# Gated DeltaNet trunk on one core: merge products later in the order, copies off GpSimd, the memory norm moved to K's and V's eviction

## The chip, the core and the metric

One core of one Trainium2 chip runs the whole kernel. Its engines are TensorE (PE; its weight loads are shown as PEld), VectorE (DVE), ScalarE (ACT), GpSimd (POOL) and SyncE (SP), which issues the DMAs. The metric is the device time of one launch in microseconds (us), lower is better.

## What is computed

Two decoder layers over 512 positions of 1024 channels, all float32. Layer 0 mixes tokens with gated DeltaNet, layer 1 with a Conformer convolution; each then cross-attends into a fixed memory of 256 positions and applies a squared-ReLU MLP. The parts that the change touches:

```python
# gated DeltaNet, 8 heads of 128, chunks of 64 positions
qkv = silu(causal_depthwise_conv(h @ w_in[:, :3072], w_conv))      # 4 taps
a_mat = eye(64) + where(strict, (k*beta) @ k.T * decay, 0)
sol = triangular_solve(a_mat, concat([v*beta, k*beta*exp(g_cum)]))
...                                                                # a scan over chunks carries the state
o = rms(o) * out_norm * silu(z);  h = h + o @ w_out
# memory cross-attention
kv = (rms_norm(mem, xa_mem_norm) ) @ w_kv                          # K and V of 256 memory positions
```

## The kernel before

Activations lie with the channels on the partitions, 128 channels by 512 positions per tile. Every float32 product is done as three matmuls in a split form: an operand is split into a high and a low part (`split`, L264; `wsplit`, L203, for weights: an ACT copy makes `wh`, DVE subtracts to make `wl`), and `mm3` (L227) multiplies high by high, high by low and low by high.

**Order.** The DeltaNet stage is written as a list of "mains" (L1136 to L1166), pieces of TensorE work that are issued one after another, and a table of "sides": `S.at(i, rank, f)` (L281) has `f` issued behind main `i`, lower ranks first. Mains 0 to 3 are the first key head and the gates' columns; then, for heads 0 to 3 (group 0) and heads 4 to 7 (group 1), come projections of k, q, z and v (`DN_ORDER`), two mains for each head; the 16 units of the cross-attention's K and V (`kv_unit`, L779) are mains 66 to 81. The places of the sides are constants by hand (`MG`, `FS`, `REC`, `K2`, ..., L1317 to L1346). A tile framework turns the issue order into one instruction order for each engine when the kernel is built: an instruction that its own reckoning has ready may go ahead of earlier ones. On the chip each engine then works its list in that fixed order and waits at the head of it.

**One group of heads.** `ev_k`, `ev_q`, `ev_v` evict a projection from PSUM (a multiply by the norm's `rb` on DVE) and apply the four convolution taps in `conv_head` (L441): tap 0 on ACT, of the others the first `npool` as an ACT multiply into `cvq` and a GpSimd add, the rest as a DVE multiply-add. v used npool 3. `k2` makes the lower-triangular matrices, `fs_in` (L517) copies their 32x32 diagonal blocks into `DB` on ACT, `fs_begin` and `fs_steps` (L527, L535) solve them by forward substitution on DVE, 31 steps of two instructions (`fst`, `X`). `fs_end` (L545) transposes the result twice into `TB` and `UB`. `mg_pre` (L554) clears `x0`, `u0` and the diagonal blocks of `bt` on GpSimd; `mg_a` (L563) copies the blocks of `TB` into `x0` on ACT and those of `UB` into `u0` on GpSimd, four copies of 32x128 each for a head. `mg_w`, `mg_y`, `mg_y`, `mg_end` (L574 to L599) are the merge products on TensorE that join the four 32-blocks to a 128-block inverse `U`. `v2` (L612) transposes v, and `rec` (L636) runs the recurrence over four 128-position chunks, three steps each, with `o_gate` and `o_norm` behind it. `head_out` (L719) transposes a head's output for the output projection "do".

**Around it.** `mem_stat` (L748) makes the memory's inverse norm `rs` and GpSimd multiplied the four memory tiles by it; `mem_gain` (L762) then applies the gain and splits. The output projection ran behind the mains (L1247 to L1260): 8 tiles `m`, each over all 8 heads. In the Conformer (L978), `CONV_SEQ` and `CONV_AFTER` place DVE's taps, their transposes ("d", `turn`), the layer norm ("l") and its output transposes ("o", `ln_out`) among the 16 K and V units of layer 1.

Of the kernel before, what the change touches and what calls it, by code (L numbers as in the profile page):

```python
# [8 lines left out]
F32 = mybir.dt.float32  # L9
# [5 lines left out]
P = 128  # L15
# [23 lines left out]
def tile_trunk(ctx, tc, xT, memT, prm_d, adt_d, bdw_d, tap_d, fin_d, w_ab, w_kq, w_v, w_z, w_dno, w_pw1, w_pw2,  # L39
# [29 lines left out]
    def tt(e, o, a, b, op):  # L69
        e.tensor_tensor(out=o, in0=a, in1=b, op=op)  # L70

# [59 lines left out]
    ind = const([P, 4], "ind")  # L131
    dve.tensor_reduce(out=ind, in_=ident.rearrange("p (x c) -> p c x", c=4), op=ALU.add, axis=AX.X)
    headm = const([P, 8], "headm")
    headx = const([P, 32], "headx")
    dve.tensor_reduce(out=headx, in_=ident.rearrange("p (x c) -> p x c", c=4), op=ALU.add, axis=AX.X)
    dve.tensor_reduce(out=headm, in_=headx.rearrange("p (a h) -> p h a", h=8), op=ALU.add, axis=AX.X)
    eps_rms = const([P, 1], "eps_rms")
# [65 lines left out]
    def wsplit():  # L203
        u = ws["split"]
        ws["split"] += 1
        while ws["load"] <= u:
            wload()
        raw = ws["raw"].pop(u)
        h = wp.tile([P, 1024], F32R, tag="wh", name=nm("wh"), bufs=NW)
        lo = wp.tile([P, 1024], F32R, tag="wl", name=nm("wl"), bufs=NW)  # L210
        act.copy(h, raw)  # L211
        (kind, i, *j), hf = order[u]
        gp = kind == "pw1" or j and kind in "KV" and i == 1 and hf == 0
        tt(pool if gp else dve, lo, raw, h.bitcast(F32), ALU.subtract)
        ws["hl"][u] = (h, lo)
# [120 lines left out]
    class DeltaNet:  # L336
# [66 lines left out]
        def decay_const(self, gq):  # L403
            if gq == 0:
                self.R = slot(F32R, "R")
# [34 lines left out]

        def conv_head(self, ps, ti, npool):  # L441
            raw = wp.tile([P, 542], F32, tag="cv", name=nm("cv"), bufs=NCV)
            pool.memset(raw[:, 0:3], 0.0)
            tt(dve, raw[:, 3:515], ps, self.n.rb, ALU.mult)
            w = [pc("w_conv", ti * 4 + j) for j in range(4)]
            a = slot(s="cva")
            act.activation(a, raw[:, 0:512], AF.Copy, scale=w[0])
            for j in range(1, 4):
                if j <= npool:
                    b = slot(s="cvq")  # L450
                    act.activation(b, raw[:, j:j + 512], AF.Copy, scale=w[j])
# [8 lines left out]
        def ev_k(self, h):  # L460
            self.KT[h] = self.conv_head(self.ps.pop(("k", h)), 8 + h, CONV_K)

        def ev_q(self, h):
            self.M["q", h] = self.conv_head(self.ps.pop(("q", h)), h, CONV_Q)

# [51 lines left out]
        def fs_in(self, h):  # L517
# [26 lines left out]

        def fs_end(self, gq):  # L545
            X = self.fs.pop(gq)[1]
            UB = fsp.tile([P, 1024], F32, tag="fs", name=nm("UB"))
            TB = fsp.tile([P, 1024], F32, tag="fs", name=nm("TB"))
            dve.transpose(out=TB, in_=X.rearrange("p (i j) -> p j i", j=32))
            dve.transpose(out=UB, in_=X)  # L550
            self.fs[gq] = UB.rearrange("p (i n) -> p n i", n=32), TB.rearrange("p (i n) -> p n i", n=32)

# [9 lines left out]

        def mg_a(self, h):  # L563
            UBv, TBv = self.fs[h // 4]
            u0, x0, bt = self.M[h]
            n = slice(h % 4 * 4, h % 4 * 4 + 4)
            for b in range(4):
                bs = slice(32 * b, 32 * b + 32)
                act.copy(c4(x0)[bs, :, bs], TBv[bs, n, :])
                pool.tensor_copy(c4(u0)[bs, :, bs], UBv[bs, n, :])  # L570

# [30 lines left out]
        def ev_v(self, h):  # L602
            self.VT[h] = self.conv_head(self.ps.pop(("v", h)), 16 + h, CONV_V)

# [31 lines left out]
        def rec(self, gq, c, step):  # L636
# [8 lines left out]
            if step == 0:  # L645
                r = self.VB[gq, c]
                if c > 0:
# [100 lines left out]
    def mem_stat():  # L748
        ps = psum("mssq")
        for i in range(2):  # L750
            pe.matmul(ps[:, 0:256], ones, mem["acc"][:, i * 256:(i + 1) * 256], start=i == 0, stop=i == 1)
        sd = slot(s="msd")
        act.activation(sd[:, 0:256], ps[:, 0:256], AF.Sqrt, bias=eps_rms, scale=1.0 / 1024)
        rs = slot(s="mrs")
        dve.reciprocal(rs[:, 0:256], sd[:, 0:256])
        mem["n"] = []
        for m in mem["m"]:
            tt(pool, m.rearrange("p (k t) -> p k t", k=2), m.rearrange("p (k t) -> p k t", k=2),
               over_c(rs[:, 0:256], 2), ALU.mult)
            mem["n"].append(m)  # L760

    def mem_gain(layer, half):  # L762
# [3 lines left out]
        for j in (2 * half, 2 * half + 1):  # L766
            mh = slot(F32R, "mh")
            ml = slot(F32R, "ml")
            for i in range(2):
                ks = slice(i * 256, (i + 1) * 256)  # L770
                src = mem["n"][j][:, ks]
                g = pc(gn, 2 * j + i)
# [6 lines left out]
    def kv_unit(layer, u):  # L779
# [3 lines left out]
        if u < 8:  # L783
# [4 lines left out]
            if hf == 1:  # L788
                K.append(split(mem["ps"], "K"))
        else:  # L790
# [5 lines left out]
            if v % 4 == 3:  # L796
                for mt in range(2):
                    V[mt, g] = split(mem["ps"][mt], "V")

# [377 lines left out]
    for h in range(8):  # L1177
        uk = max(at["k", h] + 1, T_STAT + 2)
        for u, ev, d, key, lag in ((uk, D.ev_k, D.KT, h, LAG[0]), (at["q", h] + 1, D.ev_q, D.M, ("q", h), LAG[1]),
                                   (at["v", h] + 1, D.ev_v, D.VT, h, LAG[2])):  # L1180
            S.at(u, 4, ev, h)
            S.at(u + lag, 4.1, D.silu, d, key)
# [17 lines left out]
    for gq in range(2):  # L1200
        f0, nf = FS[gq]
        S.at(f0, 5, D.fs_begin, gq)
        for i in range(nf):
            S.at(f0 + i, 6, D.fs_steps, gq, i * 31 // nf, (i + 1) * 31 // nf)
        S.at(f0 + nf, 0, D.fs_end, gq)
        S.at(f0 + 1, 7, D.norm_k, gq)
        for i in range(4):
            h = 4 * gq + i
            m = MG[gq] + i * MSTEP[gq] // 2
            S.at(m, 1, D.mg_a, h)  # L1210
            S.at(f0 + nf - 4 + i, 5, D.mg_pre, h)
            for j, f in enumerate((D.mg_w, D.mg_y, D.mg_y, D.mg_end)):
                S.at(m + 1 + j, 1, f, h)
        for c in range(4):
            S.at(max(at["v", 4 * gq + 3] + V2[gq], f0 + nf), 3, D.v2, gq, c)
        n = 0
# [7 lines left out]
    for j in range(4):  # L1224
        S.at(MEM + 3 + j, 7, mem_square, j)
    S.at(MEM + 9, 3, mem_stat)
    S.at(at["kv"] - MGAIN, 6, mem_gain, 0, 0)
    S.at(at["kv"] - MGAIN + 1, 6, mem_gain, 0, 1)
    os_, xres = [], []
    for i in range(4):  # L1230
        S.at(HO + i, 6, lambda i=i: os_.append(D.head_out(i)))
    S.at(REC[1] + 6, 8, lambda: xres.extend(load_x()))
    run(mains, S)
# [9 lines left out]

    def do_w(m):
        return wnext(("do", m // 2), m % 2), psum("do")

    w0, p0 = do_w(0)  # L1247
    proj(w0, os_, p0, 0, 4)
    w1, p1 = do_w(1)
    proj(w1, os_, p1, 0, 4)  # L1250
    for i in range(4, 8):
        os_.append(D.head_out(i))
    proj(w0, os_, p0, 4, 8)
    do_ev(0, p0)
    proj(w1, os_, p1, 4, 8)
    do_ev(1, p1)
    for m in range(2, 8):
        w, ps = do_w(m)
        proj(w, os_, ps)
        do_ev(m, ps)  # L1260
    n2 = Norm("mlp_norm0")
# [18 lines left out]
    def finish(hid, cur):  # L1280
# [3 lines left out]
        for c, g in LAST:  # L1284
# [14 lines left out]
            if g == 0:  # L1299
# [43 lines left out]
CONV_AFTER = [(3, ("t", 5)), (11, ("d", 0)), (12, ("c", 4, 0, 1)), (13, ("c", 4, 2, 3)), (13, ("t", 6)),  # L1343
              (14, ("c", 5, 0, 1, 2, 3)), (14, ("t", 7)), (15, ("d", 1)), (16, ("c", 6, 0, 1, 2, 3)), (18, ("d", 2)),
              (18, ("c", 7, 0, 1, 2, 3)), (21, ("d", 3)), (21, ("l", 0))]
CONV_AFTER += [(24 + _m, ("o", _m)) for _m in range(8)]  # L1346

# [40 lines left out]
def _layout(np, i):  # L1388
# [25 lines left out]
    r["w_z"] = _pack_b(np, w[:, 3072:4096])  # L1414
    r["w_dno"] = _pack_a(np, i["dn_w_out"][0])
    r["w_pw1"] = _pack_a(np, i["cv_w_pw1"][0], [m for h in range(8) for m in (h, 8 + h)])
# [26 lines left out]
```

## Time and profile before

| what | value |
|---|---|
| median of 3 runs (lowest to highest) | 1579.48 us (1578.74 to 1582.63) |
| the profiled execution: its time / the span of its instructions | 1581.38 us / 1579.7 us |
| mean granted TensorE clock | 0.983 of full speed |
| DVE busy / ACT busy / POOL busy | 879.1 us / 655.7 us / 237.1 us |
| DeltaNet stage with K and V of layer 0 | 0 to about 370 us |
| output projection, cross-attention, MLP of layer 0 | about 370 to 880 us |
| Conformer with K and V of layer 1 | about 880 to 1075 us |

A time in the views of the trace counts from the first instruction. "L578 PE" is an instruction that line 578 issues on TensorE; `xN` is a count. In the list of waits, each row has who waited, for whom, the sum in us, how often, and the longest. In the table of windows the columns are the window, its length, the busy time of PE, PEld, DVE, ACT and POOL, then the granted clock (PEclk), the DMA's share and GB/s. In a timeline a row has start, duration, engine, line, operation, tiles and shape, and in brackets the idle time of that engine just before and what ended it.

### The profile page before, as it was taken

To read this page: it belongs to the slowest core of one execution; us is meant where nothing else is said; L and a number is where in the kernel's file an instruction comes from. 1 tells how busy PE (TensorE), PEld (TensorE's weight loads), DVE (VectorE), ACT (ScalarE), POOL (GpSimd) and SP (SyncE) were. 2 spreads that over 40 slices of the span, in tenths; PEclk is the share of its full clock that TensorE was granted. 3 is DMA by queue.
4 is the path that set the end of the run, shared out by engine and by line. 5 is a ranking of instruction groups with operands and counts; after the bars stand their busy time and mean duration, and the time that the engine had idled before them with its cause. 6 is when DMAs were issued, how large, how long until landed. Compare 5 with 4: busy or idle time off the path is not lost.

```text
span 1579.7 us, 19402 instructions
## 1 busy us (share of the span) xinstructions
PE 1535.3 (97%) x7622; PEld 1293.8 (82%) x7622; DVE 879.1 (56%) x1296; ACT 655.7 (42%) x1003; POOL 237.1 (15%) x262
## 2 busy tenths in 40 slices
PE   7998997999999999999999999999999999999998
PEld 5886885898888888888888888978888888888887
DVE  5886878566455444343435499864545443433441
ACT  5655573745344433231324332264444432322332
POOL 1226124502111100000001541212112000000000
PEclk8999999799999999999999999999999999999999
DMA  4221112153221233233224534542213232223231
GB/s 153 81 78 51 60 50 97 51 176 107 93 67 59 89 107 94 94 97 103 93 94 158 171 126 130 181 140 96 80 40 99 92 103 95 94 97 103 93 107 54
DMA packets 51115, 156.17 MB, mean 99 GB/s; under 512 B 6608, under 2 KB 8912, under 8 KB 51024
## 3 DMA queue, kind: packets, MB, share of 16 engines
q1 hardware_dynamic: 51024, 154.93, 30.0%
q8 instruction: 60, 0.98, 0.2%
q14 instruction: 31, 0.25, 0.0%
HBM read 151.76 MB, written 2.10 MB: 97 GB/s over the span
## 4 chain that ended last, share of the span: by engine, by line
PE 78%; DVE 10%; ACT 4%; issue 2%; POOL 2%; DMA 2%; SPq 1%; DVEq 0%; POOLq 0%; ACTq 0%
PE up L229 7%; PE up L231 7%; PE up L230 7%; PE dn L231 6%; PE dn L229 6%; PE dn L230 6%; DVE ca L73 3%; PE q L229 2%; PE xo L230 2%; PE q L231 2%; PE q L230 2%; PE xo L231 2%; PE xo L229 2%; PE pw L229 1%; PE pw L230 1%
## 5 line engine op out<-in xcount | busy, mean ns | idle before, releaser
L211 ACT CAST wh<-raw 128x1024 fp32r<-128x1024 f32 x248 | 260.5, 1051 | 688.8 <-PE dn L230 190.4
L70 DVE TENSOR_TENSOR wl<-raw,wh 128x1024 fp32r<-128x1024 f32 x224 | 276.7, 1236 | 123.5 <-ACT wh L211 122.2
L229 PE MATMUL up<-xh,wh 128*128 128x512 f32 x512 | 200.4, 391 | 0.0
L231 PE MATMUL up<-xh,wl 128*128 128x512 f32 x512 | 199.4, 389 | 0.0
L230 PE MATMUL up<-xl,wh 128*128 128x512 f32 x512 | 199.4, 389 | 0.0
L230 PE MATMUL dn<-ul,wh 128*128 128x512 f32 x448 | 174.4, 389 | 0.0
L231 PE MATMUL dn<-uh,wl 128*128 128x512 f32 x448 | 174.4, 389 | 0.0
L229 PE MATMUL dn<-uh,wh 128*128 128x512 f32 x448 | 174.4, 389 | 0.0
L70 DVE TENSOR_TENSOR h<-dn,h 128x512 f32<-128x512 f32 x56 | 41.8, 747 | 163.3 <-PE dn L231 163.3
L73 DVE SCALAR_TENSOR_TENSOR rl<-up,rb 128x512 f32<-128x512 f32 x64 | 44.2, 691 | 157.0 <-PE up L231 157.0
L70 POOL TENSOR_TENSOR sq<-sq,sq 128x512 f32<-128x512 f32 x30 | 50.2, 1674 | 468.7 <-ACT sq L304 468.7
L230 PEld LDWEIGHTS up<-xl,wh 128*128 128x128 f32 x512 | 96.2, 188 | 20.3 <-issue 0.5
L229 PEld LDWEIGHTS up<-xh,wh 128*128 128x128 f32 x512 | 96.1, 188 | 20.2 <-issue 0.5
L231 PEld LDWEIGHTS up<-xh,wl 128*128 128x128 f32 x512 | 96.1, 188 | 20.1
L230 PEld LDWEIGHTS dn<-ul,wh 128*128 128x128 f32 x448 | 84.1, 188 | 17.5
L231 PEld LDWEIGHTS dn<-uh,wl 128*128 128x128 f32 x448 | 84.1, 188 | 17.4
L229 PEld LDWEIGHTS dn<-uh,wh 128*128 128x128 f32 x448 | 84.1, 188 | 17.3
L73 DVE SCALAR_TENSOR_TENSOR ca<-x,prm,ca 128x512 f32<-128x512 f32 x120 | 88.0, 750 | 3.0 <-ACT ca L1024 1.2
L229 PE MATMUL h<-xh,wh 128*128 128x512 f32 x192 | 78.6, 409 | 2.1 <-ACT xh L297 2.1
L230 PE MATMUL h<-xl,wh 128*128 128x512 f32 x192 | 77.0, 401 | 2.0 <-DVE xl L73 2.0
L231 PE MATMUL h<-xh,wl 128*128 128x512 f32 x192 | 76.1, 396 | 0.0
L70 POOL TENSOR_TENSOR wl<-raw,wh 128x1024 fp32r<-128x1024 f32 x24 | 57.6, 2404 | 117.6 <-ACT wh L211 117.6
(330 smaller groups left out, 3073.2 us busy)
## 6 DMA issues: line engine op xcount, KB each, us to landing
raw<-w_up SPq DMA_DIRECT2D x64, 512.0 KB, 3.6
raw<-w_dn SPq DMA_DIRECT2D x64, 512.0 KB, 3.6
raw<-w_pw SPq DMA_DIRECT2D x24, 512.0 KB, 3.9
tap<-tap SPq DMA_DIRECT2D x36, 256.0 KB, 5.3
raw<-w_kq SPq DMA_DIRECT2D x16, 512.0 KB, 3.6
raw<-w_k SPq DMA_DIRECT2D x16, 512.0 KB, 4.4
raw<-w_vv SPq DMA_DIRECT2D x16, 512.0 KB, 3.7
raw<-w_q SPq DMA_DIRECT2D x16, 512.0 KB, 3.6
```

The costliest lines, as they stand in the source:

```text
L70: e.tensor_tensor(out=o, in0=a, in1=b, op=op)
L73: dve.scalar_tensor_tensor(out=o, in0=a, scalar=s, in1=b, op0=op0, op1=op1)
L211: act.copy(h, raw)
L229: pe.matmul(ps, wh, xh, start=first, stop=False)
L230: pe.matmul(ps, wh, xl, start=False, stop=False)
L231: pe.matmul(ps, wl, xh, start=False, stop=last)
```

## The change

- **Solve's end.** `fs_end` and `mg_a` are split by result: first `TB` and the copies into `x0`, now on DVE; then `UB` and the copies into `u0`, now on ACT. Both are issued right behind the last solve step (mains 29 and 58; `mg_a` was at 32 and at 61 to 63).
- **Merge products** start behind main 35 (were 33) and 67 (were 62 to 64), and each pair of heads one main later. For group 1 they so stand behind the first K units.
- **v.** `conv_head` is cut into eviction (`conv_raw`) and taps (`conv_taps`). v's taps are issued at `TAPV` (33 to 35, 66 and 67); npool for v is 1, 1, 0, 0 by head. `v2` moves from mains 36 and 67 to 39 and 71, the recurrence from 39 and 68 to 42 and 73.
- **Recurrence.** `Se` goes from GpSimd to four ACT instructions, `vn` from DVE to four ACT instructions. The `DB` copies of group 1 go from ACT to DVE.
- **Memory norm.** The four GpSimd multiplies go. The gains work on the raw memory; K's eviction multiplies by the inverse norm on DVE and then splits; V's eviction takes it as the scale of ACT's and DVE's split. Four matmuls with one output column each are added to have the norm by position. Squares go from mains 56 to 59 to mains 59 to 62, the gains four mains earlier.
- **Output projection.** It is split in two halves: heads 0 to 3 as eight mains behind the V units, added into the residual `xres` on DVE; heads 4 to 7 behind the mains. The weights are packed accordingly.
- **Start.** Three DVE reduces (L132 to L136) go to main 5. The weight splits 1 to 3 keep their place in the issue order.
- **Conformer.** The last `turn` and the layer norm move two units later (21 to 23), the outputs from 24 to 31 to 26, 27, 28, 29, 30, 30, 31, 31.

```diff
-        act.copy(h, raw)
+        ins = [act.copy(h, raw)]
+        if 0 < u < 4:
+            tc.keep_in_program_order(ins[0])
...
-        def conv_head(self, ps, ti, npool):
+        def conv_raw(self, ps):
             raw = wp.tile([P, 542], F32, tag="cv", name=nm("cv"), bufs=NCV)
             pool.memset(raw[:, 0:3], 0.0)
             tt(dve, raw[:, 3:515], ps, self.n.rb, ALU.mult)
+            return raw
+
+        def conv_taps(self, raw, ti, npool):
...
-                act.copy(db[bs, :, n:n + 4], bt[bs, :, bs].rearrange("p c i -> p i c"))
+                (dve.tensor_copy if gq else act.copy)(db[bs, :, n:n + 4], bt[bs, :, bs].rearrange("p c i -> p i c"))
...
+        def fs_end(self, gq, i):
+            X = self.fs[gq][-1]
+            t = fsp.tile([P, 1024], F32, tag="fs", name=nm("UB" if i == 0 else "TB"))
+            dve.transpose(out=t, in_=X.rearrange("p (i j) -> p j i", j=32) if i else X)
+            self.fs[gq] = {i: t.rearrange("p (i n) -> p n i", n=32), -1: X}
...
-        def mg_a(self, h):
+        def mg_a(self, h, i):
+            src, dst, n = self.fs[h // 4][i], self.M[h][i], slice(h % 4 * 4, h % 4 * 4 + 4)
             for b in range(4):
                 bs = slice(32 * b, 32 * b + 32)
-                act.copy(c4(x0)[bs, :, bs], TBv[bs, n, :])
-                pool.tensor_copy(c4(u0)[bs, :, bs], UBv[bs, n, :])
+                (dve.tensor_copy if i else act.copy)(c4(dst)[bs, :, bs], src[bs, n, :])
...
+        def tap_v(self, h):
+            self.VT[h] = self.conv_taps(self.M.pop(("v", h)), 16 + h, CONV_V[h])
...
-                        tt(pool, c4(Se), c4(self.S[gq]), over_i(hcv(egl, gq, c)), ALU.mult)
+                        for i, h, isl in hs:
+                            act.activation(Se[:, isl], self.S[gq][:, isl], AF.Copy, scale=egl[:, 4 * h + c:4 * h + c + 1])
...
-                tt(dve, c4(vn), c4(ps), over_i(hcv(self.s_neg if c else self.s_all, gq, c)), ALU.mult)
+                for i, h, isl in hs:
+                    act.activation(vn[:, isl], ps[:, isl], AF.Copy,
+                                   scale=(self.s_neg if c else self.s_all)[:, 4 * h + c:4 * h + c + 1])
...
+        mem["rs"] = slot(s="mrs")
+        dve.reciprocal(mem["rs"][:, 0:258], sd[:, 0:258])
...
-                K.append(split(mem["ps"], "K"))
+                kf = slot(s="kf")
+                tt(dve, kf.rearrange("p (k t) -> p k t", k=2), mem["ps"].rearrange("p (k t) -> p k t", k=2),
+                   over_c(mem["rs"][:, 0:256], 2), ALU.mult)
+                K.append(split(kf, "K"))
...
-    S.at(0, 4, D.decay_const, 0)
+    S.at(T_STAT + 3, 1, D.decay_const, 0)
...
+        for i in (1, 0):
+            S.at(f0 + nf, 2 - i, D.fs_end, gq, i)
+            for h in range(4 * gq, 4 * gq + 4):
+                S.at(f0 + nf, 2 - i, D.mg_a, h, i)
...
+            S.at(TAPV[h], 5, D.tap_v, h)
             for j, f in enumerate((D.mg_w, D.mg_y, D.mg_y, D.mg_end)):
-                S.at(m + 1 + j, 1, f, h)
+                S.at(MG[gq] + j + i // 2, 1, f, h)
...
+    def do_first(m):
+        ps = do_mm(0, m)
+        tt(dve, xres[m], ps, xres[m], ALU.add)
+
+    at["do"] = len(mains)
+    for m in range(8):
+        mains.append(lambda m=m: do_first(m))
...
+    for m in range(8):
+        do_ev(m, do_mm(1, m))
...
-CONV_K, CONV_Q, CONV_V = 0, 1, 3
+CONV_K, CONV_Q, CONV_V = 0, 1, (1, 1, 0, 0, 1, 1, 0, 0)
...
-MSTEP = (0, -1)
-MG = (32, 63)
-V2 = (4, 3)
-MGAIN = 4
+MG = (35, 67)
+V2 = (7, 7)
+MGAIN = 8
 HO = 76
-REC = (39, 68)
+REC = (42, 73)
 MEM = 53
+MSQ = 59
+TAPV = (33, 33, 34, 35, 66, 66, 67, 67)
```

More of the change, by code (lines that the diff above doesn't have):

```diff
@@ L404, in decay_const @@
             if gq == 0:
+                dve.tensor_reduce(out=ind, in_=ident.rearrange("p (x c) -> p c x", c=4), op=ALU.add, axis=AX.X)
+                hx = small(32)
+                dve.tensor_reduce(out=hx, in_=ident.rearrange("p (x c) -> p x c", c=4), op=ALU.add, axis=AX.X)
+                dve.tensor_reduce(out=headm, in_=hx.rearrange("p (a h) -> p h a", h=8), op=ALU.add, axis=AX.X)
                 self.R = slot(F32R, "R")
@@ L751, in mem_stat @@
             pe.matmul(ps[:, 0:256], ones, mem["acc"][:, i * 256:(i + 1) * 256], start=i == 0, stop=i == 1)
+        for mt in range(2):
+            for i in range(2):
+                o = i * 256 + mt * P
+                pe.matmul(ps[:, 256 + mt:257 + mt], mem["acc"][:, o:o + P], ones[:, 0:1], start=i == 0, stop=i == 1)
         sd = slot(s="msd")
[L753 to L760, printed above, removed]
+        act.activation(sd[:, 0:258], ps[:, 0:258], AF.Sqrt, bias=eps_rms, scale=1.0 / 1024)
+        mem["rs"] = slot(s="mrs")
+        dve.reciprocal(mem["rs"][:, 0:258], sd[:, 0:258])
     def mem_gain(layer, half):
@@ L1181, in tile_trunk @@
             S.at(u, 4, ev, h)
-            S.at(u + lag, 4.1, D.silu, d, key)
+            S.at(TAPV[h] + lag if d is D.VT else u + lag, 5.1 if d is D.VT else 4.1, D.silu, d, key)
     for gq in range(2):
@@ L1242, in do_ev @@
         n1.add(m, hn)
[L1244 to L1250, printed above, removed]
     for i in range(4, 8):
         os_.append(D.head_out(i))
[L1253 to L1260, printed above, removed]
+    for m in range(8):
+        do_ev(m, do_mm(1, m))
     n2 = Norm("mlp_norm0")
@@ L1344 @@
               (14, ("c", 5, 0, 1, 2, 3)), (14, ("t", 7)), (15, ("d", 1)), (16, ("c", 6, 0, 1, 2, 3)), (18, ("d", 2)),
-              (18, ("c", 7, 0, 1, 2, 3)), (21, ("d", 3)), (21, ("l", 0))]
-CONV_AFTER += [(24 + _m, ("o", _m)) for _m in range(8)]
+              (18, ("c", 7, 0, 1, 2, 3)), (23, ("d", 3)), (23, ("l", 0))]
+CONV_AFTER += [(_i, ("o", _m)) for _m, _i in enumerate((26, 27, 28, 29, 30, 30, 31, 31))]
 def _tiles_a(np, w):
```

57 lines of the change are left out of this document (27 added, 30 removed).

## The prediction

> **What bounds the kernel now.** I read the page's first part, then who TensorE waits for, then the windows and timelines around those waits.
>
> ```profile
> span 1579.7 us, 19402 instructions
> PE 1535.3 (97%) x7622; PEld 1293.8 (82%) x7622; DVE 879.1 (56%) x1296; ACT 655.7 (42%) x1003; POOL 237.1 (15%) x262
> ```
>
> TensorE is busy for all but 1579.7 - 1535.3 = 44.4 us. The change leaves its matmuls as they are, so it can win only idle time and the slow clock that follows it. The list of waits of TensorE, whole rows, longest first:
>
> ```profile
> PE mg L578 <- POOL msq L70: 11.2, 1, 11.2
> PE mg L578 <- ACT x L569: 6.8, 2, 6.5
> PE mg L590 <- POOL cva L70: 3.2, 1, 3.2
> PE ssq L315 <- DVE sq L70: 2.8, 1, 2.8
> PE cvT L1041 <- ACT ca L1030: 2.3, 1, 2.3
> ...
> PE lnT L1088 <- DVE cy L79: 1.9, 2, 1.5
> ...
> PE vt L615 <- DVE u L70: 1.4, 1, 1.4
> ```
>
> The merge products (mg) wait 11.2 + 6.8 + 3.2 = 21.2 us. Behind each long wait the granted clock is low:
>
> ```profile
> 26.00:30.00 4.00, 4.00 (x16) 3.32 (x16) 0.95 (x3) 1.55 (x2) 0.00 (x0) 0.59 0.37 131
> 135.00:140.00 5.00, 4.93 (x24) 4.80 (x24) 0.33 (x1) 4.83 (x12) 4.62 (x9) 0.57 0.00 0
> 276.00:285.00 9.00, 8.13 (x34) 7.26 (x35) 0.00 (x0) 8.77 (x18) 8.20 (x18) 0.50 0.01 2
> 295.00:300.00 5.00, 2.35 (x16) 2.21 (x17) 5.00 (x7) 4.92 (x11) 2.46 (x2) 0.64 0.00 0
> 300.00:310.00 10.00, 10.00 (x83) 9.57 (x82) 5.40 (x12) 4.72 (x9) 3.83 (x3) 0.67 0.33 107
> 1024.00:1027.00 3.00, 3.00 (x16) 3.00 (x16) 2.74 (x10) 0.71 (x2) 0.86 (x1) 0.53 0.40 146
> 1035.00:1040.00 5.00, 3.63 (x10) 2.78 (x11) 4.66 (x8) 3.10 (x4) 0.22 (x1) 0.71 0.36 105
> ```
>
> Busy time times (1 - clock) estimates what the slow clock costs. Start: 4.0 x 0.41 = 1.6. Group 0: 4.93 x 0.43 = 2.1. Group 1: 4.1 + 0.8 + 3.3 = 8.2. Conformer: 1.4 + 1.1 = 2.5. With the idle times, the pots are: **start** 2.8 + 0.7 (below) + 1.6 = 5.1; **group 0** 6.5 + 1.4 + 2.1 = 10.0; **group 1** 11.2 + 0.3 + 3.2 + 8.2 = 22.9; **Conformer** 2.3 + 1.9 + 2.5 = 6.7. Together 45 us.
>
> **Group 0.** The timelines of TensorE, DVE, ACT and GpSimd:
>
> ```profile
> 127.99 0.39 PE L230 MATMUL h<-xl,wh 128*128 128x512 f32 x1
> 128.22 0.39 PE L231 MATMUL h<-xh,wl 128*128 128x512 f32 x1
> 135.07 4.94 PE L578 MATMUL mg<-x,bt 128*128 128x96 f32 x24 [6.46 <-ACT x L569]
> ...
> 114.36 0.39 DVE L70 TENSOR_TENSOR X<-X,fst 128x231 f32<-128x231 f32 x1
> 116.22 1.37 DVE L70 TENSOR_TENSOR X<-X,fst 128x220 f32<-128x220 f32 x1
> 128.19 1.28 DVE L70 TENSOR_TENSOR fst<-FT,X 128x60 f32<-128x60 f32 x1
> 131.69 1.94 DVE L549 STREAM_TRANSPOSE TB<-X 128x1024 f32<-128x1024 f32 x1
> 133.67 6.78 ACT L569 COPY x<-TB 32x128 f32<-32x128 f32 x16 [0.23 <-DVE TB L549]
> 115.90 1.44 POOL L70 TENSOR_TENSOR cva<-cva,cvq 128x512 f32<-128x512 f32 x1 [22.49 <-ACT cvq L451]
> ```
>
> TensorE has nothing left but merge products at 128.6; TB exists at 133.6 and ACT copies `x0` until 140.5. Two solve steps of the same size take 0.39 and 1.37 us: the slow one runs beside GpSimd's tap add. The rows at 116.2 and 128.2 are the first and the last of six solve instructions that are slow in this way, some 6 us. The change does three things here. The products come two mains later; a main is 12 matmuls, and in the timeline they start 0.23 us apart, so 5.4 us. v's taps leave the solve's window, where GpSimd's adds fall from 12 to 2; I take 4 of the 6 us, since v's remaining taps are DVE work that can be slipped in between solve steps. And `x0` is copied on DVE:
>
> ```profile
> 36.21 0.22 DVE L360 COPY abt<-abT 128x64 f32<-128x64 f32 x1
> ...
> L73 DVE SCALAR_TENSOR_TENSOR cva<-cv,prm,cva 128x512 f32<-128x512 f32 x40 | 32.2, 806 | 13.4 <-POOL cva L70 9.1 <-ACT cva L447 3.9
> L687 ACT ACTIVATE oq<-qS,egd 128x128 f32<-128x128 f32 x24 | 6.8, 369 | 4.4 <-PE qS L684 4.4
> L70 DVE TENSOR_TENSOR cv<-h,rb 128x512 f32<-128x512 f32 x24 | 16.3, 681 | 5.8 <-ACT rb L327 3.3 <-PE h L231 2.5
> ```
>
> No row shows a DVE copy of 32x128; between 0.22 (DVE's nearest copy) and 0.42 (ACT's 6.78 / 16) I take 0.22, the same engine: 16 are 3.5 us. TB is then done at 129.6 and `x0` at 133.1, TensorE comes at 128.6 + 5.4 = 134.0: no wait. Late next is `u0`: UB and a weight split or two are done at about 136, and 16 ACT copies of 0.42 end at 143, the first heads' at 139; the second product comes at 134.0 + two heads' first products (16 of the 24, at full clock 4.94 x 0.57 x 16 / 24 = 1.9) + a main (2.7) = 138.6. I leave 2 us of waits with a little slow clock: **gain 8** of 10.0.
>
> **Group 1.** TensorE, DVE and ACT, and a window of K units:
>
> ```profile
> 264.98 0.39 PE L231 MATMUL h<-xh,wl 128*128 128x512 f32 x1
> 276.54 1.99 PE L578 MATMUL mg<-x,bt 128*128 128x96 f32 x8 [11.17 <-POOL msq L70]
> ...
> 267.48 1.90 DVE L549 STREAM_TRANSPOSE TB<-X 128x1024 f32<-128x1024 f32 x1
> 274.99 0.63 ACT L458 ACTIVATE cva<-cva 128x512 f32<-128x512 f32 x1 [5.10 <-POOL cva L70]
> ...
> 315.00:320.00 5.00, 5.00 (x45) 5.00 (x44) 2.67 (x4) 1.89 (x2) 0.00 (x0) 1.00 0.32 108
> ```
>
> The wait is booked on GpSimd's msq, but ACT's row says more: ACT stands 5.1 us at the silu of a v tap that GpSimd has not added, with the copies to `x0` behind it. The change takes the copies from that queue and puts three v mains (8.2 us) and two K units (24 matmuls each; 45 in 5.0 us, so 2.7) ahead of the products: TensorE comes at 265.4 + 8.2 + 5.4 = 279.0. DVE gets more to do before: `DB` copies 3.5, the recurrence's last chunk now three mains later (some 3), slipped-in taps (4 x 0.81) and gains (8 at half of 0.81, 3.3); less 3 to 6 of slow steps. Net some 6: TB's end at 275.4, the first two heads' `x0` at 277.2, all at 279: no long wait. But mains 66 to 73 (22 us of K units and some 6 of merge products) then hold 28 us of DVE work: 8 weight splits at 1.2, 10 taps at 0.81, K evictions 5, 12 merge adds 5. I leave 6 us for waits at `u0`, the v transposes and their slow clock: **gain 17** of 22.9. K's gains read the raw memory, so K waits for no norm.
>
> **Start.** DVE's reduces stand ahead of the first `xl`, and a weight split ahead of the last square's add, which releases ssq at 25.7:
>
> ```profile
> 8.93 0.38 DVE L132 TENSOR_REDUCE ind<-ident 128x4 f32<-128x128 f32 x1
> ...
> 9.66 0.54 DVE L70 TENSOR_TENSOR abp<-wab,abp 128x128 fp32r<-128x128 f32 x1
> ...
> 23.87 1.22 DVE L70 TENSOR_TENSOR wl<-raw,wh 128x1024 fp32r<-128x1024 f32 x1
> ```
>
> Without the reduces the first `xl` is 9.66 - 8.93 = 0.7 earlier. With splits 1 to 3 in issue order, the squares come ahead and the sum is there before TensorE asks. **Gain 5.** The reduces cost 0.9 at main 5; that is nothing while DVE is less than a main (2.7) late there, and 0.9 if it is later.
>
> **Conformer.** The last `turn` comes two K units later (5.4 us), and DVE's taps gain 3 us of work from four K evictions (0.68 each), so the 2.3 and its slow clock go. The layer norm's wait stays or grows: its distance to the first output is three units as before, now all V units. **Gain 3.5** (0 to 6).
>
> **The rest.** The new K evictions (8 x 0.68), `do_first` (8 x 0.68) and `vn`, `Se` (4 x 0.37 each on ACT) lie beside matmuls; their cover is a main of 2.7 us. If the cover of K's were gone, they would cost 0.7 for each. The four norm matmuls cost 0.5. DMA count and bytes stay; the x loads move on SP by four mains, with four left before use. **Sum:** 5 + 8 + 17 + 3.5 - 0.5 = 33. The profiled execution took 1581.4, 1.9 above the median of the runs; taken from the median: 1579.5 - 33 = 1546.5, rounded to **1547**.
>
> **Two rules.** The Trainium skill, "TensorE: Matmul & The Clock Gate", Part 1, says that the clock halves after an idle window of about 3.4 us; by that, the short waits that I leave would cost only themselves, some 3 us less in all, and the time 1544 (an estimate by that page). The trace differs: the wait of 2.3 us at cvT is followed by a clock of 0.53. I keep the row. The Trainium skill, "SBUF — State Buffer", section "Who interferes with whom", says that DVE with two SBUF inputs and a reading GpSimd exclude each other, with which the solve steps above agree; it adds that a DVE copy in a two-port mode excludes GpSimd altogether, which speaks against copies on DVE, and which no row of these shapes shows.
>
> **The rivals.**
> - *The solve of group 1 ends later still*: all of DVE's added work (`DB` 3.5, `x0` 3.5, taps 8, gains 3, recurrence 3) falls ahead of the products, about 20 us behind 267.5; TensorE waits some 10 us again with the slow clock, and this pot yields 4: 1547 + 13 = 1560. For it: issue places are only priorities, so taps and gains may be slipped in between solve steps. Against: GpSimd's slow steps go.
> - *The products are pulled forward*: the build moves them ahead by its own reckoning, as it did with the mg row at 276.54, which stands ahead of a v main's matmuls. Pots of 10.0 and 22.9 yield 5 and 8: 1559.
> - *DVE's copies wait for GpSimd*: five GpSimd reads (three memory squares, two tap adds) of 1.4 us (the tap add above) fall into the copies of group 1, 7 us and 2 of slow clock: 1556. This is what the second rule above would do.
> - *Nothing comes of it*: each wait is replaced by one for `u0` or for v behind the later taps: 1579.
> - *Slower*: the recurrence waits for ACT.
>
> ```profile
> 335.20 0.89 PE S L673 x8
> 336.09 0.89 PE qS L684 x8
> ...
> L211 ACT CAST wh<-raw 128x1024 fp32r<-128x1024 f32 x248 | 260.5, 1051 | 688.8 <-PE dn L230 190.4
> ```
>
> `vn` now queues on ACT behind `Se` (1.5) and a weight copy (1.05): 4.0 us with its own 1.5, against a cover of a main, S and qS (2.7 + 1.8 = 4.5). From 0.5 us more in the queue TensorE waits; at 3.5 us on each of 8 chunks, and 1.5 of slow clock behind each, it costs 40: 1586. It decides above 4.1 a chunk. Against: ACT's `oq` in the same chain makes no wait today.
>
> **How the numbers follow.** Forecast 0.60 (own range 1536 to 1555: 11 better if nearly all pots empty, 8 worse if half the u0 and Conformer terms fail); late solve 0.15, pulled forward 0.06, copies waiting 0.04, nothing 0.05, slower 0.10. The range takes the forecast and the three partial cases, with the floor of all 45 us (1534): 1534 to 1566. What a measurement of this kernel can tell from no change is 0.3%, 5 us: faster 0.60 + 0.25 = 0.85, same 0.05, slower 0.10.
>
> **What would show it.** TensorE's waits at L578 below 2 us each; no slow solve step beside a tap add; ssq's wait gone; clock 1.00 between 130 and 310; cvT's wait gone, lnT's still there. I am wrong if L590, vt or `o` waits take their place, if TB of group 1 ends over 10 us later against TensorE, or if K waits for `ml`.

## The result, and the profile after

The changed kernel takes **1567.3 us** (median of 6 runs, 1563.2 to 1567.4) against 1579.8 us (6 runs, 1578.7 to 1582.6): a ratio of 0.991, 95% interval 0.990 to 0.9925, so 12.5 us faster. The forecast was 1547 in a range of 1534 to 1566. The sign came out, the size did not: 13 of 33 us. The profile's first part:

```profile
span 1565.7 us, 19421 instructions
...
PE 1530.1 (98%) x7630; PEld 1289.4 (82%) x7630; DVE 903.2 (58%) x1372; ACT 653.3 (42%) x1017; POOL 186.6 (12%) x202
```

GpSimd lost 50 us of work, DVE took on 24, ACT's stayed. TensorE is 5.2 us less busy with the same matmuls and the norm's four small ones more, two records each (mean granted clock 0.987, 0.983 before), but 35.6 us of the span are still idle on it, 44.4 before. The list of TensorE's waits says where (who waited, for whom: us in total, times, longest):

```profile
PE mssq L759 <- POOL msq L70: 13.7, 1, 13.7
PE h L229 <- ACT xh L297: 3.1, 1, 3.1
PE mg L592 <- ACT w L582: 2.5, 2, 1.6
PE lnT L1102 <- DVE cy L79: 2.5, 2, 1.9
PE ct L418 <- DVE grep L416: 1.6, 1, 1.6
PE S L681 <- DVE vnd L70: 1.3, 1, 1.3
...
PE vn L668 <- DVE r L73: 1.0, 1, 1.0
```

All long waits of the merge products (11.2, 6.8 and 3.2 before) are gone, and so are those for ssq and cvT. In their place stands one wait of 13.7 us that no part of the prediction speaks of: `mssq`, the two sums of the memory's norm. The timelines around it, DVE, then ACT, GpSimd and TensorE:

```profile
256.62 2.11 DVE L555 STREAM_TRANSPOSE TB<-X 128x1024 f32<-128x1024 f32 x1
...
259.77 4.48 DVE L572 COPY x<-TB 32x128 f32<-32x128 f32 x16
259.95 6.74 ACT L572 COPY u<-UB 32x128 f32<-32x128 f32 x16 [2.52 <-DVE UB L555]
266.72 0.91 ACT L780 ACTIVATE mh<-mem,prm 128x256 fp32r<-128x256 f32 x2
267.53 1.03 ACT L207 CAST wh<-raw 128x1024 fp32r<-128x1024 f32 x1
268.47 1.70 ACT L780 ACTIVATE mh<-mem,prm 128x256 fp32r<-128x256 f32 x4
270.07 2.17 ACT L750 ACTIVATE msq<-mem 128x512 f32<-128x512 f32 x4
271.29 4.34 POOL L70 TENSOR_TENSOR msq<-msq,msq 128x512 f32<-128x512 f32 x3 [4.38 <-ACT msq L750]
275.68 2.08 PE L759 MATMUL mssq<-msq,ones 128*128 128x256 f32 x4 [13.71 <-POOL msq L70]
277.54 1.71 PE L763 MATMUL mssq<-ones,msq 128*128 128x1 f32 x8
```

Read it from below. TensorE's wait is booked on GpSimd's add, but GpSimd itself had been idle for 4.4 us and waited for ACT's squares; the squares were waiting for nothing but their turn, behind 16 copies to `u0`, six gains and a weight copy. At the head of that list ACT had itself stood idle for 2.5 us, until `UB` was there. `x0`, the result that the merge products had waited for before, was ready at 264.3. The windows after it, PE's busy time second and the granted clock ahead of the DMA share:

```profile
270.00:275.00 5.00, 0.00 (x0) 0.00 (x0) 1.82 (x3) 3.53 (x6) 3.56 (x3) 0.50 0.35 104
275.00:280.00 5.00, 4.33 (x16) 3.97 (x17) 0.20 (x1) 0.71 (x2) 0.62 (x1) 0.50 0.01 2
280.00:285.00 5.00, 5.00 (x27) 5.00 (x27) 4.15 (x4) 2.76 (x5) 2.55 (x3) 0.55 0.00 0
```

Wait and slow clock together are 13.7 + 4.33 x 0.50 + 5.00 x 0.45 = 18.1 us. Without both, and if nothing else had come late, the profiled run would have taken about 1549 (an estimate; e1 and e2 show what else was late).

To see what each part gave, I cut the span at five marks that lie in the same order in all kernels: the start of the first z matmul, of the last z matmul of group 1, of the last "do", of the first "pw" and of the last "dn". Lengths in us, one profiled execution each:

| kernel | start | group 0 | group 1, recurrence, do | layer 0's rest | Conformer, layer 1 |
|---|---|---|---|---|---|
| before | 78.3 | 170.4 | 166.2 | 465.9 | 692.8 |
| changed | 75.6 | 164.2 | 162.9 | 465.8 | 691.1 |
| e1 squares early | 75.4 | 161.2 | 154.9 | 465.8 | 690.9 |
| e2 squares, gains early | 74.8 | 161.2 | 157.1 | 465.8 | 689.7 |
| e3 gains early | 75.5 | 162.8 | 156.9 | 465.7 | 689.4 |
| e4 sum behind the first K | 74.6 | 161.2 | 159.7 | 465.8 | 690.7 |
| e5 = e2, v taps later | 75.8 | 162.7 | 151.4 | 465.8 | 690.7 |
| e6 = e5, group 0 and ct too | 72.0 | 158.3 | 151.2 | 465.8 | 691.0 |
| e7 Conformer as before | 74.6 | 162.8 | 162.1 | 465.8 | 692.7 |
| e8 start as before | 78.9 | 165.2 | 162.0 | 465.9 | 690.7 |
| e9 = e6, u0 later | 71.6 | 158.2 | 151.3 | 465.7 | 691.0 |
| e10 = e9, outputs later | 72.1 | 158.3 | 151.8 | 465.8 | 687.4 |
| e11 vn, Se as before | 75.0 | 161.2 | 161.3 | 465.7 | 691.3 |
| e12 u0 on GpSimd | 74.0 | 164.6 | 158.4 | 465.7 | 691.0 |

So the change gave 2.7, 6.2, 3.3 and 1.7 us, where the prediction had 5, 8, 17 (less 0.5 for the rest) and 3.5. Rows with the same code in a column differ by up to 3 us (group 0: the changed kernel 164.2, e4 161.2); the last section says why.

### The profile page after: what moved, and what is told of

Same layout as the page of the kernel before. It is cut to its first block, busy times and chain, and to the rows that moved or that the text cites. A ratio compares the mean times of both kernels' runs of the same rounds, so it can differ in the third digit from the quotient of the medians.

```text
span 1565.7 us, 19421 instructions
## 1 busy us (share of the span) xinstructions
PE 1530.1 (98%) x7630; PEld 1289.4 (82%) x7630; DVE 903.2 (58%) x1372; ACT 653.3 (42%) x1017; POOL 186.6 (12%) x202
## 4 chain that ended last, share of the span: by engine, by line
PE 89%; DVE 6%; ACT 1%; issue 1%; DMA 1%; SPq 1%; POOL 0%; ACTq 0%; POOLq 0%; DVEq 0%
PE up L229 7%; PE up L230 7%; PE up L231 7%; PE dn L230 6%; PE dn L229 6%; PE dn L231 6%; PE pw L229 3%; PE pw L231 3%; PE pw L230 3%; PE q L229 2%; PE xo L230 2%; PE q L230 2%; PE xo L231 2%; PE q L231 2%; PE xo L229 2%; PE h L230 1%
```

## The experiments

Each time is a median, with its ratio to the kernel before and the 95% interval. Theory A is that `mssq` stands in TensorE's fixed order and waited for squares which queued on ACT behind `u0`; the rivals are named in the expectations.

**e1: only the squares earlier.**

```diff
-    S.at(MSQ + 5, 3, mem_stat)
+    S.at(64, 3, mem_stat)
...
-MEM = 53
-MSQ = 59
+MEM = 49
+MSQ = 52
```

> The changed kernel with the memory's load and squares moved ahead (load from main 53 to 49, squares from mains 59-62 to 52-55), so that ACT makes the squares before the copies to u0; the norm's sum (mssq) stays at main 64 and the gains stay where they are. Theory A: TensorE's wait of 13.7 us at mssq came from the squares queued on ACT behind the u0 copies (259.95 to 266.72) and the gains (to 270.17); with the squares early that wait is gone. The next late thing in A are the gains themselves, half of which still stand behind u0 (to 270.2): K's first unit waits about 5 to 8 us for mh, with half clock, instead of starting at 279.1. So 8 to 10 us better than the changed kernel: about 1558 (1555 to 1561). Rival B: mssq's wait stands in front of another one that ends at the same time (u0, x0 or the merge products), and the time stays within 3 us of 1567. Rival C: the three GpSimd adds (4.3 us) are what is long, not ACT's queue: 4 us better, 1563.

1556.9 us, ratio 0.985 (0.984 to 0.987): 10 us better than the changed kernel. Group 1 has 8.0 us of the difference between the two profiles; another 3.0 lie in group 0's column and come from the clock (last section). The list of waits has no `mssq` any more, but two new rows, and the timeline has it at 255.88 without a wait:

```profile
PE K L230 <- DVE ml L73: 3.9, 1, 3.9
...
PE K L229 <- ACT mh L780: 1.1, 1, 1.1
```

Theory A holds, and in the size that the next late thing allowed: K's first unit waits for the gains, the half of them that still stands behind `u0`. Rival B (another wait that ends at the same time) falls: group 1 takes 8.0 us less (162.9 to 154.9). Rival C falls too, since GpSimd's three adds were kept.

**e2: squares and gains earlier; e3: only the gains.** e2 sets MSQ to 56 and MGAIN to 11, e3 MGAIN alone.

> The changed kernel with squares (mains 59-62 to 56-59) and gains (mains 58, 59 to 55, 56) both issued earlier, so that in ACT's order all eight gains and all four squares stand ahead of the u0 copies; mssq stays at main 64. Theory A: nothing that TensorE needs between main 64 and the first merge product is then behind u0; mssq and K's first units have no long wait, and the 13.7 us with their 4 us of slow clock are won: about 1550 (1547 to 1554). Rival B: the wait moves to the merge products (x0, u0) or to K's eviction, which needs the norm's root from ACT, now behind u0 too: above 1560. Rival C: as the squares alone, 1558, if gains behind u0 cost nothing.

> The changed kernel with only the gains three mains earlier; the squares stay at mains 59-62 and behind u0. Theory A: the squares come forward only by the gains that stood between (six of 0.43 to 0.46, from 270.1 to 267): mssq at about 272.5 instead of 275.7, and the wait 10.5 instead of 13.7: about 1563 (1561 to 1565). Rival C (only the gains were late, mssq would have waited for nothing without them): about 1552. Rival B: no change.

e2: 1556.0 us, 0.985 (0.9835 to 0.986). e3: 1559.5 us, 0.987 (0.9855 to 0.989). The two are nearly one kernel, 3.5 us apart by the medians and 1.8 by the profiles: with the gains out of the way the build pulled e3's squares ahead of `u0` by itself (ACT makes them at 255.82 and the `u0` copies at 266.18), and `mssq` waits 0.7 us in both. So e3 did not separate gains from squares as meant. And e2 is not the 1550 that theory A gave. Its list of waits (of the first row, 3.4 us are in group 1):

```profile
PE mg L592 <- ACT w L582: 5.8, 3, 3.4
PE K L231 <- DVE wl L70: 3.7, 3, 1.8
```

Rival B was half right: the wait moved on, though not to above 1560. Rival C's number came out (e2 takes what e1 takes) but not its reason: K's waits for the gains, 5.0 us in e1, are gone, and others stand in their place. Two timelines of e2 show to where, DVE's solve and ACT ahead of the second merge product:

```profile
254.88 1.23 DVE L70 TENSOR_TENSOR fst<-FT,X 128x87 f32<-128x87 f32 x1
256.14 1.33 DVE L70 TENSOR_TENSOR X<-X,fst 128x87 f32<-128x87 f32 x1
...
254.71 4.00 POOL L70 TENSOR_TENSOR msq<-msq,msq 128x512 f32<-128x512 f32 x3 [6.71 <-ACT msq L750]
...
279.59 1.28 ACT L465 ACT_TABLE_LOAD   x1
280.88 0.63 ACT L465 ACTIVATE cva<-cva 128x512 f32<-128x512 f32 x1
281.42 0.85 ACT L582 ACTIVATE w<-mg 128x384 f32<-128x384 f32 x2
```

The square adds now run beside the end of the solve, whose steps take 1.2 to 1.3 us in place of 0.25 (the same two in e1), and the gains' `ml` are slipped into the solve as well: TB starts 24.6 us behind the last z matmul, 16.8 in the changed kernel. No merge product waits for `x0` because of it. Behind that, ACT stands at a table load and a silu of v's taps while the merge products need `w`.

**e4: the sum behind the first K unit.** `mem_stat` at main 66 instead of 64.

> The changed kernel with mssq and the root behind the first K unit (main 66) instead of main 64; squares and gains are untouched. Theory A: TensorE then waits for the gains instead (they end at 270.2 behind u0), does one K unit of 2.7 us in the time in which GpSimd adds, and asks for mssq at about 273 to 274 against 275.6: the start of the second K unit comes 2.5 to 5 us earlier: about 1563 (1561 to 1565). Rival: if K needs no gain of the late half at once, and mssq alone is late, the K unit fills 262 to 265 and the wait shrinks by all of its length plus clock: 1560 or better.

1560.2 us, 0.988 (0.986 to 0.989), 7 us better by the medians. Some 3 of these lie in group 0 (161.2 against 164.2) and come from the clock; group 1 itself gained 3.2, within the 2.5 to 5 that theory A gave. The median is also the number of the rival (1560), but its mechanism is not there: the first K unit does wait for the gains, 2.8 and 1.6 us, and `mssq` for another 2.1. The same work in another order gave another wait.

**e5: v's taps of group 1 behind the merge products; e6: the same for group 0, and ct's operand earlier.** e5 is e2's gains with e1's squares, and

```diff
-V2 = (7, 7)
-REC = (42, 73)
-TAPV = (33, 33, 34, 35, 66, 66, 67, 67)
+V2 = (7, 10)
+REC = (42, 75)
+TAPV = (33, 33, 34, 35, 69, 69, 70, 70)
```

e6 adds TAPV 35, 35, 36, 36 for group 0 with its transposes and recurrence one main later, and makes the copy `grep` at main 6 instead of main 10.

> Squares as in e1 (mains 52-55, load 49), gains as in e2 (mains 55, 56), and group 1's v taps three mains later (66, 67 to 69, 70), the v transposes and the recurrence of group 1 behind them (71 to 74, 73 to 75). In e2 the long wait moved to the second merge product: TensorE waited 5.8 us for w, and ACT stood at the silu of a v tap ahead of that copy. Theory A2 (what stays of the loss in group 1 is ACT's queue again, now the taps ahead of w, and GpSimd's square adds beside the solve): w's wait in group 1 goes, the solve has no slow step beside msq, K's waits for weight parts stay at about 3 us: 1549 (1546 to 1552). Rival: the taps and their silus then delay the v transposes or the recurrence, or the u0 copies hold the weight copies: 1555 or more.

> e5 and the same for group 0 (v taps at mains 35, 35, 36, 36 instead of 33 to 35, transposes and recurrence one main later), and the DVE copy grep of the decay sums four mains earlier than its matmul. Theory A2: group 0's two waits for w (0.9 and 1.6 us) and the wait of 1.6 us at ct go, with a slow clock behind them of 0 to 3.5 and 0 to 1.7 us: 2 to 5 us better than e5, about 1546. Rival: the taps come too late for the v transposes, which then wait, or taps run into group 1's evictions: no better than e5, or slower.

e5: 1552.5 us, 0.9825 (0.981 to 0.984), between the 1549 of its theory and the 1555 of its rival: the wait for `w` in group 1 is gone and group 1 is at 151.4, but K now waits 4.0 us at `wl`. e5 changes two things against e2: the place of the squares, and that of the taps with what hangs on them. Its solve tells them apart: with the squares early it still has a slow step (1.49 us beside a square add) and ends as late, with TB 24.4 us behind the last z.

```profile
262.90 2.09 DVE L555 STREAM_TRANSPOSE TB<-X 128x1024 f32<-128x1024 f32 x1
```

So the 5.7 us that group 1 gained over e2 (157.1 to 151.4) are not those of a faster solve; they go with the wait for `w` and its slow clock, that is with the taps. e6: **1546.2 us**, 0.979 (0.977 to 0.980), as expected. Its waits, and two windows:

```profile
PE K L231 <- DVE wl L70: 4.1, 2, 3.7
PE lnT L1105 <- DVE cy L79: 2.6, 2, 2.0
```

```profile
40.00:60.00 20.00, 19.93 (x104) 16.65 (x103) 15.35 (x26) 18.64 (x26) 2.31 (x6) 1.00 0.14 44
...
135.00:140.00 5.00, 5.00 (x44) 4.20 (x44) 3.81 (x8) 4.74 (x10) 1.96 (x4) 1.00 0.01 4
```

Neither ct nor `w` is in the whole list, and the clock is 1.00 at both places. The start column falls from 75.8 to 72.0, group 0 from 162.7 to 158.3.

**e7: the Conformer as before; e8: the start as before.** Both undo one part of the changed kernel.

> The changed kernel with the Conformer's places as before the change (last turn and layer norm at 21, outputs at 24 to 31). By the landmarks of the two traces the Conformer part gave 1.7 us (lead 12.2 us ahead of it, 13.9 behind it), against 3.5 in the prediction: 1569 (1567 to 1571), with the wait for ca (2.3 us) back. Rival: the wait at cvT went for another reason (other DVE work less): 1567, no wait back.

> The changed kernel with the start as before (three reduces at the head of DVE's list, weight splits 1 to 3 free to be reordered). By the landmarks the start gave 2.7 us at the first z (78.3 to 75.6), against 5 in the prediction, and a new wait of 1.6 us at ct with some slow clock took part of it. If that wait came with the reduces' new place, it goes here: the ssq wait of 2.8 us comes back with its clock, ct's wait goes, 1570 (1568 to 1572). If ct's wait is not theirs, it stays beside ssq's, and the time is 1572 to 1574.

e7: 1567.3 us, 0.992 (0.989 to 0.994): the median shows no difference, which is inconclusive, since 1.7 us is less than its interval can tell. The segments show it: with the old places Conformer and layer 1 take 692.7 and 692.8 us (e7 and before), with the new ones 689.4 to 691.3 in the eleven kernels that have them (e10 moves them again), and cvT's wait is back (1.6 us). e8: 1570.2 us, 0.994 (0.992 to 0.995), 2.9 us slower, as expected; the wait for ssq is back (3.6 us) and the one at ct is gone. So the new wait at ct belongs to the start's own part; which of its two moves made it, e8 does not say.

**e9: u0 of group 1 later; e10: the layer norm's outputs later, too.** e9 is e6 with `u0` issued at mains 66 and 67, e10 is e9 and

```diff
-CONV_AFTER += [(_i, ("o", _m)) for _m, _i in enumerate((26, 27, 28, 29, 30, 30, 31, 31))]
+CONV_AFTER += [(_i, ("o", _m)) for _m, _i in enumerate((27, 28, 29, 30, 30, 31, 31, 31))]
```

> e6 with the u0 copies of group 1 issued at mains 66 and 67 instead of 58, so that one weight copy of K goes ahead of the last five of them in ACT's order. In e6 the longest wait left between 250 and 330 is 3.7 us of K at wl: ACT makes that unit's wh at 264.49, behind 16 u0 copies of 6.76 us, and DVE's wl follows behind the reciprocal and an eviction. If ACT's copies hold it: wh comes 2.1 us earlier (5 copies of 0.42) and the wait falls to about 1.6 us with less slow clock: 1543.5 (1542 to 1546). If DVE's own queue (x0 copies 4.6, reciprocal 1.8, eviction 0.6) holds wl, nothing changes: 1546.

> e9 with the Conformer's outputs one unit later (27 to 31 instead of 26 to 31). The layer norm's wait (2.6 us at lnT for cy, and a clock of 0.90 to 0.93 behind it) is that of a DVE chain that ends too late: one unit of 2.7 us more takes most of it: 2 to 3 us better than e9, 1541. Rival: the outputs then crowd behind the last unit and what TensorE gains it waits for there: no better than e9.

e9: 1547.0 us, 0.979 (0.978 to 0.980): nothing gained. The list of waits still has K's 3.7 us at `wl`, and the timelines of ACT and DVE say which queue held it:

```profile
261.92 1.04 ACT L207 CAST wh<-raw 128x1024 fp32r<-128x1024 f32 x1
...
257.08 4.67 DVE L575 COPY x<-TB 32x128 f32<-32x128 f32 x16
261.78 1.77 DVE L770 RECIPROCAL mrs<-msd 128x258 f32<-128x258 f32 x1
263.46 0.63 DVE L70 TENSOR_TENSOR cv<-h,rb 128x512 f32<-128x512 f32 x1
264.00 2.35 DVE L70 TENSOR_TENSOR wl<-raw,wh 128x1024 fp32r<-128x1024 f32 x2
```

ACT's `wh` was at 264.49 in e6 and is at 261.92 here (with all of e9 0.5 us earlier at this place), and DVE still made `wl` at the same point of its own list, behind the `x0` copies, the reciprocal and an eviction: 264.47 in e6, 264.00 here. What is left there is DVE's. e10: **1543.0 us**, 0.9765 (0.975 to 0.978), the best of all, 4.0 better than e9 where 2 to 3 were expected: the wait at lnT falls from 2.5 to 0.6 and the last column from 691.0 to 687.4.

**e11: vn and Se as before; e12: u0 on GpSimd.** Again one part each of the changed kernel.

> The changed kernel with vn on DVE and Se on GpSimd, as before the change. In the trace of the changed kernel the recurrence of group 1 has new waits (S for vnd 1.3 us, vn for r 1.0 us), 43.68 us busy of 45. If ACT's new instructions cause them (the direction of the prediction's slower rival, by two small waits instead of 40 us): they go, 1565 (1563 to 1566.5). If they come from DVE's load at the recurrence's new place: they stay or grow, since DVE gets vn back, 1567 to 1569.

> The changed kernel with the u0 copies on GpSimd, as before the change, beside the x0 copies on DVE. Two things are told apart. First, ACT then has gains and squares free of u0 (the squares would be done at about 262 instead of 272), but GpSimd's three square adds stand behind its 16 u0 copies. If only ACT's queue mattered, mssq's wait shrinks by 8 us or more: 1557. If the queue merely moves to GpSimd (16 copies of 0.39, to about 266, and 4.3 of adds): mssq at about 271, 5 us less: 1561. Second, x0 beside GpSimd copies: if the two engines hinder each other, 16 x0 copies take 6 us or more in place of 4.5, and GpSimd's more than 6.2, and the time stays at 1565 or above.

e11: 1563.9 us, 0.989 (0.988 to 0.991); its interval overlaps that of the changed kernel. Of the two small waits, that of S for `vnd` goes (1.3 us) and that of `vn` for `r` stays (1.2); the latter lies in group 0's recurrence, not in group 1's as the expectation has it. Between 325 and 370 TensorE's busy time rises from 43.68 to 44.86, and group 1's column falls by 1.6, so `vn` and `Se` on ACT cost some 1.2 to 1.6 us; the rest of the medians' difference lies in group 0's column.

e12: 1562.9 us, 0.989 (0.9875 to 0.990). Its timelines of ACT, DVE, GpSimd and TensorE:

```profile
258.51 2.18 ACT L750 ACTIVATE msq<-mem 128x512 f32<-128x512 f32 x4
...
258.54 6.84 DVE L572 COPY x<-TB 32x128 f32<-32x128 f32 x16
265.40 6.34 DVE L73 SCALAR_TENSOR_TENSOR ml<-mem,prm,mh 128x256 fp32r<-128x256 f32 x8
...
258.75 6.92 POOL L572 COPY u<-UB 32x128 f32<-32x128 f32 x16 [13.48 <-DVE UB L555]
...
266.15 4.13 POOL L70 TENSOR_TENSOR msq<-msq,msq 128x512 f32<-128x512 f32 x3
...
270.33 2.08 PE L759 MATMUL mssq<-msq,ones 128*128 128x256 f32 x4 [9.61 <-POOL msq L70]
```

The squares are done at 260.7, 11.5 us earlier, and `mssq` still waits 9.6 us, because the queue in front of the sum is now GpSimd's: the `u0` copies stand ahead of the adds. It is the same lateness in another queue, 4 us smaller, which is the second case named. What was asked beside it came out apart from the time: the `x0` copies beside GpSimd's took 6.84 us in place of 4.48, but TensorE asked for `x0` only after `mssq`, so that it cost nothing here.

## Why the prediction was right in direction and wrong in size

- **The step that failed** is in group 1: "K's gains read the raw memory, so K waits for no norm", and with it "no long wait" and a gain of 17. K's matmuls need no norm, but the matmuls that *make* the norm stand in TensorE's fixed order ahead of K's first unit. I followed the data that K needs and not the list that TensorE works through. The diff had all of it: the squares were moved three mains later, 16 copies were moved to ACT, and I charged those copies to `u0`'s users alone: `u0` is issued at main 58, the squares at 59 to 62, and `mssq` at 64. The term of 17 us so gave 3.3. What I should have asked of the moved squares is what I asked of `vn`: which instructions stand ahead of it on ACT, and who waits at the end. e1 shows the cause, e4 and e12 that it is order and queue. One sign that I had named, K waiting for `ml`, was hidden behind `mssq`: e1 has it, 3.9 us.
- **It was not the only thing in that pot.** With `mssq` freed, e2 fell into the waits for `w` (3.4 us in group 1) and `wl` (3.7). Its solve ended later too, but e5's ended as late and group 1 was 5.7 us faster, so what e5 won back had been lost in ACT's queue, as at `mssq`. e5 and e6 won 11.5 and 11.7 us over the changed kernel in group 1: 15 of the 22.9 us pot. That is near the 17 and not all of it, and it took v's taps behind the products.
- **DVE's sum in group 1** was wrong as well, without deciding the time. The terms listed come to 13.0, less 3 to 6, so 7 to 10 and not "some 6". Measured, TB ended 10.7 us earlier than before: 8.9 of these because TensorE came to the same place that much earlier, and 1.8 against TensorE's work, where 6 later was forecast. The rival of a later solve so did not happen in the changed kernel; the later solve came in e2 and e5.
- **Start**, 5 predicted, 2.7 gained: the mechanism was right (ssq's wait went; e8 brings it back), the term was short of a new wait. `decay_sums` came late in DVE's list: its input was there at 40.3, but `grep` stood behind seven conv taps until 47.3, 1.6 us late for TensorE with 1.6 of slow clock behind it. I had priced the reduces at main 5 as their own 0.9 us, and not what comes behind. With `grep` earlier (e6) the start column is 6.3 us below before.

```profile
42.64 4.72 DVE L73 SCALAR_TENSOR_TENSOR cva<-cv,prm,cva 128x512 f32<-128x512 f32 x7
47.28 0.22 DVE L416 COPY grep<-g 128x128 f32<-128x128 f32 x1
...
47.64 0.46 PE L418 MATMUL ct<-tri_mid,grep 128*128 128x128 f32 x2 [1.65 <-DVE grep L416]
```

- **Group 0**, 8 predicted, 6.2 to 9.2 gained (164.2 in the changed kernel, 161.2 in e4, with one code): right. Four of the six slow solve steps went, as taken, and `x0` was ready at 128.7, before TensorE asked at 130.2. The 2 us that I left for waits were 2.5, but not at `u0`: `w` stood on ACT behind the silu of a v tap (below). This is what I had read in the profile of before for `x0`, one product further on.

```profile
133.79 0.63 ACT L465 ACTIVATE cva<-cva 128x512 f32<-128x512 f32 x1 [0.63 <-DVE cva L73]
...
135.27 0.48 ACT L582 ACTIVATE w<-mg 128x384 f32<-128x384 f32 x1
137.16 0.63 ACT L465 ACTIVATE cva<-cva 128x512 f32<-128x512 f32 x1 [1.41 <-DVE cva L73]
137.70 0.47 ACT L582 ACTIVATE w<-mg 128x384 f32<-128x384 f32 x1
```

- **Conformer**, 3.5 predicted, 1.7 gained: cvT's wait went (e7 brings it back), and lnT's grew from 1.9 to 2.5, as I had allowed. One unit more for the outputs was worth another 3.6 (e10).
- **The slower rival** was priced at 5 us for each chunk and would have decided above 4.1; `vn` and `Se` on ACT cost some 1.2 to 1.6 us in all (e11).
- **DVE's copies waiting for GpSimd** did not occur in group 1, since the build left GpSimd nothing but small memsets there (0.16 to 0.19 us): 16 copies took 4.48 us, 0.28 each, against the 0.22 that I had taken. In group 0 they took 5.50 us, mostly because one of them took 0.96 beside a GpSimd memset of 1.01; no matmul waited for it. e12 shows that the danger was real.
- **What would show it**: L578's long waits, ssq's and cvT's went, lnT's stayed, as named. "No slow solve step beside a tap add" held but for two steps: the two adds that were left still made steps of 1.35 and 1.22 us. "Clock 1.00 between 130 and 310" failed, and that is where the missing time was found. Of the signs of being wrong, the waits of L590, now L592, came in part (2.5 us, in group 0); the wait that decided, `mssq`, was not among them.

## What to carry to other kernels

When operations are moved, list every instruction in the in-order queue of the engine that bounds the kernel, the small ones too, and ask for each when its input exists; "the big matmul no longer needs it" says nothing of the small matmul in front. A wait that is booked on one engine is followed back through that engine's own wait to the queue where something stood ready and not served. And when one such wait is removed, do not count on all of it: here 18 us came back as 8 (e1), then 11.5 (e5) as the next queues were cleared.

## What the runs showed of the hardware

**The price of a short wait is a matter of chance.** In group 0 the changed kernel and e4 have the same code and the same two waits (0.9 and 1.6 us). The windows behind them, the changed kernel first:

```profile
135.00:140.00 5.00, 2.60 (x18) 2.47 (x19) 4.87 (x7) 3.31 (x8) 0.65 (x2) 0.78 0.39 107
140.00:145.00 5.00, 5.00 (x22) 4.63 (x22) 4.71 (x8) 2.12 (x5) 0.20 (x2) 0.54 0.29 102
```

```profile
135.00:140.00 5.00, 3.41 (x33) 3.27 (x33) 4.90 (x7) 2.75 (x6) 0.65 (x2) 1.00 0.45 156
140.00:145.00 5.00, 5.00 (x43) 4.16 (x42) 4.34 (x8) 2.81 (x6) 0.20 (x2) 1.00 0.15 51
```

22 matmuls in five microseconds in the one, 43 in the other: 3 us from nothing in the code. e1, with the same two waits (0.8 and 1.6 us), has 1.00 in both windows; e7, with all of this code unchanged, has 0.71 and 0.95. The changed kernel's own runs spread by as much (1563.2 to 1567.4, at mean clocks of 0.991 and 0.987), which fits, though only one of them is profiled here. The Trainium skill, "TensorE: Matmul & The Clock Gate", Part 1, has a window of about 3.4 us that runs freely, so that the point at which the clock changes depends on where in it the first matmul lands; that the same waits met different clocks agrees with it. Its condition of a whole idle window does not: here no idle stretch is over 1.6 us, and the clock still halves in some executions. I priced such clocks as certain (the pots). The three kernels with one code in group 0's column (changed, e4, e7: 164.2, 161.2, 162.8) lie 1.5 us above the lowest on average, half of the worst; that is three executions, no more.

**GpSimd's copies slowed DVE's copies, and hardly the other way.** In e12 DVE's 16 copies in group 1 took 6.84 us beside GpSimd's, 4.48 without them in the changed kernel (a median of 0.42 against 0.26 for one). GpSimd's took a median of 0.39 for one there (0.41 in group 0), and 0.39 to 0.40 before the change, where the `x0` copies were ACT's. Both ran in the same 7.1 us. Eight `ml` took 6.34 us there, beside the copies' end and the square adds, 0.79 each; four in e1 took 1.68, 0.42 each. The Trainium skill, "SBUF — State Buffer", section "Who interferes with whom", names a DVE instruction of two SBUF inputs beside a reading GpSimd, with which `ml` and the slow solve steps of e2 agree. By its rule of full exclusion for copies in a two-port mode, e12's 32 copies would have taken the sum of their times, 4.5 + 6.9 = 11.4 us (an estimate); they took 7.1. That is no proof against the rule, since no run here shows the mode that these copies ran in, nor for how much of a recorded time the ports are held, and the one copy of 0.96 us beside a memset of 1.01 in group 0 looks like exclusion.
